# Last gate projection by 128-channel columns, between seven-product steps of the out-projection's left half

## The chip, the cores and the metric

One core of a Trainium2 chip runs the whole program. The metric is device time in microseconds (us). The kernel before took 2122.43 us, the median of three runs (2122.37 to 2122.54). A profile of one execution stands beside the times.

## What is computed

A decoder trunk of two layers on 256 tokens of width 2048, all in float32. The part that the change touches is, per layer:

```python
h = _rmsnorm(x, attn_norm_g[l])
proj = h @ w_in[l]
q, k, v, gate_b, gate_c, conv_in = jnp.split(proj, splits, axis=-1)   # each 1024 wide
...
attn = (_rmsnorm(attn, subln_g[l]) * (1.0 - lam_init)).reshape(B, S, ATTN_WIDTH)
conv = gate_b * _short_conv(gate_c * conv_in, conv_w[l])
x = x + jnp.concatenate([attn, conv.astype(attn.dtype)], axis=-1) @ w_out[l]
hm = _rmsnorm(x, mlp_norm_g[l]) @ w_up[l]
x = x + jnp.square(jax.nn.relu(hm)) @ w_down[l]
```

## The kernel before

**Numbers in two halves.** Every float32 operand of a matmul is split into a rounded high half and the rest: ScalarE (ACT) copies `hi`, VectorE (DVE) subtracts to get `lo`. A product is then three matmuls (`TERMS`: hi by hi, hi by lo, lo by hi). Weights come from HBM into `raw` buffers by DMAs that SyncE (SP) issues, and are split as they arrive (lines 322 and 323, `whi` and `wlo`). There are four `raw` buffers (`RAW`) and three of each of `whi` and `wlo` (`wpool`). `Weights.take` writes the next weight tiles into the program three jobs (`AHEAD`) before they are used.

**The order.** TensorE's order is the order in which the Python code issues matmuls. The other engines' orders come from a scheduler, and buffers of a pool are handed out in the order of the code. Each engine's queue is strictly in order: an instruction that waits holds up all behind it. `work` holds background pieces (attention, norms) that advance at each `tick` between matmuls.

**The mixer of a layer.** q, k and v are projected, then `gate_c` and `conv_in` in four groups of 256 channels each (`linear_t`, line 433), with the attention of the second half of the heads between them. Then comes `gate_b` (the last gate, tiles `gb`), also in four groups of 256 channels: for each, 32 matmuls over eight blocks of channels with 512 columns (high and low half of the activations at once) and 256 columns, twice. `joined` and `gate` add the two halves, multiply by the convolution and store both halves of the result in `cat[2]` and `cat[3]`. `cat[0]` and `cat[1]` hold the attention.

**The out-projection.** `BySeven.project` runs once for the left 1024 output columns (`g` = 0) and once for the right. The contraction of 2048 rows goes in eight pairs of 128-row blocks (pairs 0 to 3 are attention, 4 to 7 the gated convolution). An ordinary pair is two chunks of 12 matmuls with 512 columns. For the pairs in `GATED` (4 and 5) the 2x2 blocks are multiplied with seven products instead of eight: 21 matmuls instead of 24. Such a step needs sums of the activations (`sums_of`, tiles `sv`, `sf`) and sums of the weights (`jobs`: tile `w7t` for the sums, `w7b`, `w7x`, `w7y` for the split halves), and four additional accumulators, which are added into `x` at the end. The MLP's first loop (line 1172, `upc`, and line 1215, `pr`) has long had columns of 128 channels and seven-product steps in turn.

**PSUM.** Eight banks: `mm2` is two tiles of two banks, `bank` is three tiles of one bank, `av` is one bank.

Of the kernel before, what the change touches and what calls it, by code (L numbers as in the profile page):

```python
# [38 lines left out]
GATED = (0, 1)  # L39
# [83 lines left out]
def trunk(ctx: ExitStack, tc: tile.TileContext, x, w_in, w_out, conv_w, q_norm_g, k_norm_g,  # L123
# [142 lines left out]
    def load_bias(l, bpool, bias, setup):  # L266

        if l == 0:
            yield from small_setup(*setup)
        revs = []  # L270
        for j in range(2):
            rev = bpool.tile([P, NH, S], F32, tag="b", name=f"rev{l}{j}")
            src = by_dist_d[j * NH:(j + 1) * NH, 0:S]
            nc.gpsimd.dma_start(
                rev, bass.AP(src.tensor, src.offset, [[1, P], [REL, NH], [1, S]]))
            revs.append(rev)
        yield 4 if l else 12
        for h in range(0, NH, 2):
            for j in range(2):
                late(nc.scalar.activation(bias[:, j * NH + h:j * NH + h + 2],  # L280
                                          revs[j][:, h:h + 2, ::-1], AF.Copy))
            yield 2
# [24 lines left out]
    class Weights:  # L307
# [80 lines left out]

        def turned(self, w, col):
            for i in range(D // P // 4):  # L390
                self.plain(w, 4 * P * i, col, 4)

# [217 lines left out]
    def attention(l, qT, kT, kL, v, h0, dst, bias, tmp, pace):  # L610
# [9 lines left out]
        def unit(i):  # L620
# [19 lines left out]
            for t in range(NT):  # L640
                W = (t + 1) * P
                for m in range(2):
                    nc.vector.tensor_tensor_reduce(
                        out=s[:, m, OFF[t]:OFF[t] + W], in0=sc[t][:, m],
                        in1=bias[:, 2 * h + m, S - W:], op0=ALU.add, op1=ALU.max, scale=1.0,
# [60 lines left out]
            yield 12 * pace  # L706
            for t in range(NT):
# [4 lines left out]
                tp3 = tp.rearrange("p (h c) -> p h c", c=P)  # L712
                hi = parts[:, 0, :, t * P:(t + 1) * P]
                nc.scalar.activation(hi, tp3, AF.Copy, scale=s_gain[:, l:l + 1])
                nc.vector.scalar_tensor_tensor(
                    parts[:, 1, :, t * P:(t + 1) * P], tp3, s_gain[:, l:l + 1], hi.bitcast(F32),
                    op0=ALU.mult, op1=ALU.subtract)
# [17 lines left out]
    def in_parts(dst, j, value):  # L735

        hi, lo = (dst.open()[:, i, 2 * j:2 * j + 2] for i in range(2))
        nc.scalar.activation(hi, value, AF.Copy)
        nc.vector.tensor_sub(lo, value, hi.bitcast(F32))
        dst.ready = j == 1  # L740

    def gate(q, acc, cv, dst, y):
        g = joined(acc, f"gb{q}")
        nc.vector.tensor_mul(y, g, cv[:, q * 2:q * 2 + 2])
        in_parts(dst, q % 2, y)
# [5 lines left out]
    class BySeven:  # L751
# [3 lines left out]
        def __init__(self, l, bpool, weights):  # L755
            self.l, self.pool, self.weights = l, bpool, weights
            n = D // (4 * P)
            seven = [n + q for q in GATED]
            plain = [i for i in range(2 * n) if i not in seven]


            self.orders = []
            for g in range(2):
                chunks = (2 * g, 2 * g + 1)
                order = [(n, i) for n in chunks for i in plain[:2]]
                for i, j in zip(plain[2:], seven):
                    order += [("seven", j), ("pair", i)][::-1 if g else 1]
                order += [("pair", i) for i in plain[2 + len(seven):-2]]
                order += [(n, i) for n in chunks for i in plain[-2:]]
                self.orders.append(order)  # L770
            self.sums = []

        def sums_of(self, q, y):

            if len(self.sums) % 2 == 0:
                room = self.pool.tile([P, 2, 2, 4, P], F32R, tag="b", name="sf")
                self.sums += [room[:, 0], room[:, 1]]
            a11, a21, a12, a22 = (y[:, k, t * P:(t + 1) * P] for k in range(2) for t in range(NT))
            v = wide(f"sv{q}").rearrange("p (s c) -> p s c", c=P)
# [4 lines left out]
            hi, lo = (self.sums[GATED.index(q)][:, part] for part in range(2))  # L784
# [3 lines left out]
        def jobs(self, w, i, col):  # L788
# [8 lines left out]
            def two(pool, tag, name, src):  # L797

                room = pool.tile([P, 2, 2, CH], F32R, tag=tag, name=name)
# [3 lines left out]
            def plain():  # L803
# [9 lines left out]
                b11, b21 = two(self.pool, "b", "w7b", raws[0])  # L813
# [4 lines left out]
            def sums():  # L818
                left, right = mine["raw"]
                t = mine["t"] = self.pool.tile([P, 4, CH], F32, tag="b", name="w7t")  # L820
# [3 lines left out]
                made = two(apool, "a", "w7x", t[:, 0:2])  # L824
# [5 lines left out]
            def more():  # L830
                return two(apool, "a", "w7y", mine["t"][:, 2:4])
# [3 lines left out]
        def project(self, g, cat, norm, kpool, tmp):  # L835
            weights, order = self.weights, self.orders[g]
            both = [mm.tile([P, NT, CH], F32, tag="mm2", name=f"o{self.l}{2 * g + n}")
                    for n in range(2)]
            accs = [[acc[:, t] for t in range(NT)] for acc in both]
            prods = {2: accs[0][0], 4: accs[0][1], 3: accs[1][0]}  # L840

            def plain(i, n):
                hi, lo = weights.take()
                for j in range(2):
                    k = 2 * i + j
                    a = cat[k // KG]
                    while not a.ready:
                        work.tick()
                    for t in range(NT):
                        for m, (pa, pw) in enumerate(TERMS):  # L850
                            nc.tensor.matmul(  # L851
                                accs[n][t], a.ap[:, pa, k % KG, t * P:(t + 1) * P],
                                (hi, lo)[pw][:, j], start=(k == 0 and m == 0),
                                stop=(i == last and j == 1 and m == 2))
                    work.tick()

            def form(i, pa, a):
                q = i - D // (4 * P)
                if a >= S1:
                    return self.sums[GATED.index(q)][:, pa, a - S1]  # L860
                k, t = 2 * i + a // 2, a % 2
                return cat[k // KG].ap[:, pa, k % KG, t * P:(t + 1) * P]

            def seven(i, start, end):
                if start:
                    for n in (1, 5, 6):
                        prods[n] = bank(f"po{self.l}{g}{n}")
                    prods[7] = ps.tile([P, CH], F32, tag="av", name=f"po{self.l}{g}7", bufs=1)
# [3 lines left out]
                for n, a, b in ((1, A11, b11), (2, A12, b21), (3, S4, b22), (5, S1, t1),  # L872
                                (7, S3, t3), (6, S2, t2), (4, A22, t4)):
                    own = n in (1, 5, 6, 7)
                    for m, (pa, pw) in enumerate(TERMS):
                        nc.tensor.matmul(prods[n], form(i, pa, a), b[pw],
                                         start=(start and own and m == 0),
                                         stop=(end and own and m == 2))
# [4 lines left out]
            def onto(n):  # L883
                for t in range(NT):
                    nc.vector.tensor_add(xs[2 * g + n][:, t], accs[n][t], xs[2 * g + n][:, t])

            last = order[-1][1]
            steps = [i for what, i in order if what == "seven"]
            done = [j for j, (what, i) in enumerate(order) if what == 2 * g][-1]
            for j, (what, i) in enumerate(order):  # L890
                if what == "pair":
                    plain(i, 0)
                    plain(i, 1)
                elif what == "seven":
                    seven(i, i == steps[0], i == steps[-1])
                    if i == steps[-1]:

                        x11, x21, x12, x22 = (xs[2 * g + n][:, t]
                                              for n in range(2) for t in range(NT))


                        room = tmp.tile([P, 2, CH], F32, tag="ao", name="es", bufs=1)
                        e1, e2, e3 = room[:, 0], wide("e2"), room[:, 1]
                        e4 = kpool.tile([P, CH], F32, tag="kL", name="es4")
                        nc.scalar.activation(e1, prods[1], AF.Copy)
                        nc.vector.tensor_add(e2, prods[6], e1)
                        nc.vector.tensor_add(e4, prods[5], e2)
                        nc.vector.tensor_add(x22, prods[5], x22)
                        nc.vector.tensor_add(e3, prods[7], e2)
                else:  # L910
                    plain(i, what - 2 * g)
                    if j == done:
                        onto(0)
                        for x_, e in ((x11, e1), (x21, e3), (x12, e4), (x22, e3)):
                            nc.vector.tensor_add(x_, x_, e)
                        if g:
                            work.start(norm.chunk(2 * g, 2), 2)
            onto(1)
            if g:
                work.start(norm.chunk(2 * g + 1, 2))  # L920
                return
            for n in range(2):
                work.start(norm.chunk(n, 2), 4 * n + 2)


    def mixer(l, norm, loads):

        with ExitStack() as scope:
            biasp = scope.enter_context(tc.tile_pool(name="biasp", bufs=1))
# [14 lines left out]
            for q in range(AW // WC):  # L944
                weights.turned(w_in[l], 3 * AW + q * WC)
            by_seven = BySeven(l, bpool, weights)
            for g, order in enumerate(by_seven.orders):
                for what, i in order:
                    if what == "seven":
# [535 lines left out]
```

## Time and profile before

| | |
|---|---|
| median of 3 runs | 2122.43 us |
| the profiled execution's own time | 2122.24 us |
| its span, first to last instruction | 2120.4 us |
| around the span | 1.8 us |
| TensorE busy | 2115.1 us |
| VectorE busy | 1748.2 us |
| ScalarE busy | 1382.2 us |
| granted TensorE clock | 1.0 |

In the profiled execution `gate_b` of layer 0 starts at 253.2 us and ends at 297.6; the out-projection follows until 383.9. In layer 1 the same starts at 1307.7. The views give busy times per engine and stretch, groups of equal instructions with their mean duration, instructions in order of time, and each DMA's time from issue to landing. A matmul's recorded duration is longer than the distance to the next one, since matmuls overlap; distances between starts are what counts.

### The profile page before, as it was taken

To read this page: it belongs to the slowest core of one execution; us is meant where nothing else is said; L and a number is where in the kernel's file an instruction comes from. 1 tells how busy PE (TensorE), PEld (TensorE's weight loads), DVE (VectorE), ACT (ScalarE), POOL (GpSimd) and SP (SyncE) were. 2 spreads that over 40 slices of the span, in tenths; PEclk is the share of its full clock that TensorE was granted. 3 is DMA by queue.
4 is the path that set the end of the run, shared out by engine and by line. 5 is a ranking of instruction groups with operands and counts; after the bars stand their busy time and mean duration, and the time that the engine had idled before them with its cause. 6 is when DMAs were issued, how large, how long until landed. Compare 5 with 4: busy or idle time off the path is not lost.

```text
span 2120.4 us, 29268 instructions
## 1 busy us (share of the span) xinstructions
PE 2115.1 (100%) x10845; PEld 1807.6 (85%) x10845; DVE 1748.2 (82%) x2428; ACT 1382.2 (65%) x1838; POOL 159.2 (8%) x226
## 2 busy tenths in 40 slices
PE   9999999999999999999999999999999999999999
PEld 7888888888888888888888888888888888888887
DVE  6777678898888888799766776788988888888997
ACT  6776555676776776666566765557777677675664
POOL 3010100000000000011101101000000000000110
PEclk9999999999999999999999999999999999999999
DMA  8546666787777777788655565658877777777993
GB/s 279 175 154 205 193 194 191 251 257 226 230 233 233 230 236 230 248 299 293 213 169 182 162 212 179 199 169 267 258 229 235 231 232 233 231 229 261 319 309 104
DMA packets 297744, 476.02 MB, mean 224 GB/s; under 512 B 12707, under 2 KB 193781, under 8 KB 297600
## 3 DMA queue, kind: packets, MB, share of 16 engines
q1 hardware_dynamic: 269120, 406.76, 60.1%
q0 software_dynamic: 28288, 67.24, 9.9%
q8 instruction: 85, 1.39, 0.3%
q14 instruction: 59, 0.48, 0.1%
q10 hardware_dynamic: 192, 0.15, 0.0%
HBM read 440.52 MB, written 33.58 MB: 224 GB/s over the span
## 4 chain that ended last, share of the span: by engine, by line
PE 99%; ACT 1%; issue 0%; DVE 0%; DVEq 0%
PE upc L1172 31%; PE pr L1215 14%; PE dn L1296 8%; PE o L851 6%; PE ci L433 4%; PE gc L433 4%; PE gb L433 4%; PE k L408 4%; PE q L408 4%; PE v L408 4%; PE dn L1378 2%; PE dn L1215 2%; PE pr1r L1215 2%; PE pr0r L1215 1%; PE up L1172 1%; PE upw L1172 1%
## 5 line engine op out<-in xcount | busy, mean ns | idle before, releaser
L1172 PE MATMUL upc<-nT,uhi 128*128 128x512 f32 x1920 | 454.7, 389 | 0.0
L323 DVE TENSOR_TENSOR wlo<-raw,whi 128x1024 fp32r<-128x1024 f32 x258 | 311.8, 1222 | 156.9 <-ACT whi L322 85.6
L1172 PEld LDWEIGHTS upc<-nT,uhi 128*128 128x128 f32 x1920 | 360.3, 188 | 74.7
L322 ACT ACTIVATE whi<-raw 128x1024 fp32r<-128x1024 f32 x258 | 272.8, 1059 | 230.1 <-PE gb L433 28.0
L1036 DVE TENSOR_TENSOR ulo<-uraw,uhi 128x1024 fp32r<-128x1024 f32 x256 | 311.7, 1221 | 110.7 <-ACT f L1204 91.5
L1035 ACT ACTIVATE uhi<-uraw 128x1024 fp32r<-128x1024 f32 x256 | 270.6, 1057 | 157.8 <-PE upc L1172 137.5
L1172 PEld LDWEIGHTS upc<-nT,ulo 128*128 128x128 f32 x1920 | 246.2, 191 | 9.3
L1172 PE MATMUL upc<-nT,ulo 128*128 128x256 f32 x1920 | 249.1, 283 | 0.0
L1296 PE MATMUL dn<-whi,fb 128*128 128x512 f32 x496 | 156.5, 389 | 0.0
L851 PE MATMUL o<-whi,cat 128*128 128x512 f32 x384 | 122.0, 391 | 0.0
L1061 ACT ACTIVATE b2h<-draw 128x1024 fp32r<-128x1024 f32 x83 | 88.2, 1063 | 48.5 <-PE pr L1215 41.3
L322 ACT ACTIVATE whi<-uraw 128x1024 fp32r<-128x1024 f32 x62 | 65.9, 1062 | 81.8 <-PE dn L1296 66.0
L1296 PEld LDWEIGHTS dn<-whi,fb 128*128 128x128 f32 x496 | 93.1, 188 | 19.2
L1182 ACT ACTIVATE ev<-upc 128x512 f32<-128x512 f32 x120 | 72.0, 600 | 54.5 <-PE upc L1172 54.5
L1061 ACT ACTIVATE t24h<-t 128x1024 fp32r<-128x1024 f32 x83 | 88.3, 1063 | 22.8 <-PE pr L1215 15.9
L1062 DVE TENSOR_TENSOR t24l<-t,t24h 128x1024 fp32r<-128x1024 f32 x83 | 101.1, 1218 | 1.7
L1062 DVE TENSOR_TENSOR b2l<-draw,b2h 128x1024 fp32r<-128x1024 f32 x83 | 100.9, 1215 | 1.1 <-ACT b2h L1061 1.1
L1062 DVE TENSOR_TENSOR t13l<-t,t13h 128x1024 fp32r<-128x1024 f32 x83 | 101.0, 1217 | 0.7
L1075 DVE TENSOR_TENSOR t<-draw 128x1024 f32<-128x1024 f32 x83 | 101.1, 1218 | 0.3
L1061 ACT ACTIVATE t13h<-t 128x1024 fp32r<-128x1024 f32 x83 | 88.4, 1065 | 13.3 <-DVE t L1075 2.9
L1296 PE MATMUL dn<-wlo,fb 128*128 128x512 f32 x248 | 96.5, 389 | 0.0
L1215 PE MATMUL pr<-t13h,f 128*128 128x512 f32 x240 | 93.8, 391 | 0.0
(447 smaller groups left out, 4296.3 us busy)
## 6 DMA issues: line engine op xcount, KB each, us to landing
uraw<-in_w_up_dram SPq DMA_DIRECT2D x128, 1024.0 KB, 6.3
raw<-in_w_in_dram SPq DMA_DIRECT2D x191, 512.0 KB, 4.3
draw<-in_w_down_dram SPq DMA_DIRECT2D x174, 512.0 KB, 5.2
raw<-in_w_out_dram SPq DMA_DIRECT2D x64, 512.0 KB, 4.2
uraw<-in_w_down_dram SPq DMA_DIRECT2D x62, 512.0 KB, 5.7
raw<-in_w_down_dram SPq DMA_DIRECT2D x10, 1024.0 KB, 5.4
hid0p<-f POOLq DMA_DIRECT2D x19, 512.0 KB, 3.6
fb<-hid0p POOLq DMA_DIRECT2D x19, 512.0 KB, 7.5
```

The source lines that it names most:

```text
L322: pair = (nc.scalar.activation(hi, raw, AF.Copy), nc.vector.tensor_sub(lo, raw, hi.bitcast(F32)))
L323: nc.vector.tensor_sub(lo, raw, hi.bitcast(F32)))
L408: nc.tensor.matmul(acc[:, t], a.ap[:, pa, k % KG, t * P:(t + 1) * P], (hi, lo)[pw][:, j], start=(k == 0 and (pa, pw) == (0, 0)), stop=(k = ...
L433: nc.tensor.matmul(acc[:, f, 0] if part else acc[:, f], wt[:, k % 4, fs], a.ap[:, 0, k % KG] if part else a.ap[:, :, k % KG], start=(part ...
L851: nc.tensor.matmul(accs[n][t], a.ap[:, pa, k % KG, t * P:(t + 1) * P], (hi, lo)[pw][:, j], start=(k == 0 and m == 0), stop=(i == last and ...
L1035: pair = (nc.scalar.activation(hi, src, AF.Copy), nc.vector.tensor_sub(lo, src, hi.bitcast(F32)))
L1036: nc.vector.tensor_sub(lo, src, hi.bitcast(F32)))
L1061: keep(nc.scalar.activation(hi, src, AF.Copy))
L1062: keep(nc.vector.tensor_sub(lo, src, hi.bitcast(F32)))
L1172: nc.tensor.matmul(acc[:, 0] if part else acc, wt[part][:, k], a.ap[:, 0, k % KG] if part else a.ap[:, :, k % KG], start=(part == 0 and kh ...
L1215: nc.tensor.matmul(prods[n], f[:, pa, a], b[pw], start=(start and m == 0), stop=(stop and m == 2))
L1296: nc.tensor.matmul(prods[p], f[:, pa, 2 * k + t], b[pw][:, n], start=(p in starts and k == 0 and m == 0), stop=(stop and k == 1 and m == 2))
```

## The change

`gate_b` goes by columns of 128 channels (`c` 0 to 7): 16 matmuls with 512 columns and 16 with 256 for each, with two weight loads each of 1024 rows by 128 channels. Each column accumulates in one bank (`bank` for the first, `av` for all others). Between the columns stand the halves of seven-product steps of the out-projection's left half. Five pairs (0 to 4) of the left half now go by seven; the fifth (pair 4) follows the ordinary pair 5. Half `a` of a step has 12 matmuls, half `b` has 9. The order is the tuple `LEFT`. The right half keeps two such steps, of pairs 2 and 3 instead of 4 and 5. The sums of activations of pairs 0 to 3 are made at the end of each attention half, where the output now first goes through a copy (`ay`) in SBUF. The bias tile is cut in two, and its two buffers are used afterwards for `w7x` and `w7y`; `w7t` of the left half takes the buffer of `kL`, and the sums of pair 4 take two buffers of `tmp`.

```diff
-GATED = (0, 1)
+LEFT = (("c", 0), ("c", 1), ("a", 0), ("c", 2), ("b", 0), ("c", 3), ("a", 1), ("c", 4), ("b", 1),
+        ("c", 5), ("a", 2), ("c", 6), ("b", 2), ("c", 7), ("a", 3), ("b", 3), (0, 5), (1, 5),
+        ("a", 4), ("b", 4), (0, 6), (1, 6), (0, 7), (1, 7))
+SEVEN_LEFT = tuple(i for what, i in LEFT if what == "a")
+SEVEN_RIGHT = (2, 3)
...
+        def column(self, w, col):
+            def half(kh):
+                def make():
+                    raw = self.pool.tile([P, 8, P], F32, tag="raw", name="raw", bufs=RAW)
+                    nc.sync.dma_start(
+                        raw, w[kh * 8 * P:(kh + 1) * 8 * P, col:col + P].rearrange(
+                            "(k p) c -> p k c", p=P))
+                    return self.halves(raw)
+                return make
+            return [half(kh) for kh in range(2)]
...
+    def column_part(acc, acts, weights):
+        tiles = [weights.take() for _ in range(2)]
+        for part in range(2):
+            for kh, wt in enumerate(tiles):
+                for k in range(8):
+                    a = acts[kh * 2 + k // KG]
+                    nc.tensor.matmul(
+                        acc[:, 0] if part else acc, wt[part][:, k],
+                        a.ap[:, 0, k % KG] if part else a.ap[:, :, k % KG],
...
-                hi = parts[:, 0, :, t * P:(t + 1) * P]
-                nc.scalar.activation(hi, tp3, AF.Copy, scale=s_gain[:, l:l + 1])
+                y = wide(f"ay{h0}_{t}")
+                nc.scalar.activation(y, tp, AF.Copy, scale=s_gain[:, l:l + 1])
+                ys.append(y.rearrange("p (h c) -> p h c", c=P))
+                hi = parts[:, 0, :, t * P:(t + 1) * P]
+                nc.scalar.activation(hi, ys[t], AF.Copy)
+                nc.vector.tensor_sub(parts[:, 1, :, t * P:(t + 1) * P], ys[t], hi.bitcast(F32))
                 yield 2
+            for j in range(2):
+                sums_of(h0 // 2 + j, *(ys[t][:, 2 * j + k] for k in range(2) for t in range(NT)))
+                yield 2
...
+    def gate(c, acc, cv, dst, y):
+        ev = nat.tile([P, 2, S], F32, tag="wide", name=f"gb{c}")
+        nc.scalar.activation(ev, acc, AF.Copy)
+        nc.vector.tensor_add(y, ev[:, 0], ev[:, 1])
+        nc.vector.tensor_mul(y, y, cv[:, c])
+        hi, lo = (dst.open()[:, i, c % KG] for i in range(2))
+        nc.scalar.activation(hi, y, AF.Copy)
+        nc.vector.tensor_sub(lo, y, hi.bitcast(F32))
+        dst.ready = c % KG == KG - 1
...
+        def left(self, acts, cv):
+            weights, l = self.weights, self.l
+            while not self.cat[1].ready:
+                work.tick()
+            self.prods = prods = {}
+            def column(c):
+                acc = (ps.tile([P, CH], F32, tag="av", name=f"gb{l}{c}", bufs=1) if c else
+                       bank(f"gb{l}{c}"))
+                acc = acc.rearrange("p (h s) -> p h s", h=2)
+                column_part(acc, acts, weights)
...
+                gate(c, acc, cv, self.cat[2 + c // KG], y[:, c % 2])
+                if c % 2 and i in SEVEN_LEFT + SEVEN_RIGHT:
+                    self.sums_of(i, ...)
+            for j, (what, i) in enumerate(LEFT):
+                if what == "c":
+                    column(i)
+                elif what == "a":
+                    if start:
+                        banks()
+                    b11, b21, b22 = weights.take()
+                    self.t1, self.t3 = weights.take()
+                    self.product(1, i, A11, b11, start, end)
+                    self.product(2, i, A12, b21, start, not {"a", 0} & rest)
+                    self.product(3, i, S4, b22, start, not {"a", 1} & rest)
+                    self.product(5, i, S1, self.t1, start, end)
+                elif what == "b":
+                    t2, t4 = weights.take()
+                    self.product(7, i, S3, self.t3, start, end)
+                    self.product(6, i, S2, t2, start, end)
+                    self.product(4, i, A22, t4, start, not {"b", 0} & rest)
+                    if end:
+                        add = self.results(0)
+                else:
+                    opening = what == 1 and 8 not in prods
+                    if opening:
+                        prods[8] = ps.tile([P, CH], F32, tag="av", name=f"po{l}8", bufs=1)
+...
+                    self.pair(i, [(what, accs[what])], [(1, 1)] if opening else (),
+                              not {what, "b"} & rest)
+                    if j == len(LEFT) - 1:
+                        add()
+                        for n in range(2):
+                            for t in range(NT):
+                                nc.vector.tensor_add(xs[n][:, t], accs[n][t], xs[n][:, t])
...
-            biasp = scope.enter_context(tc.tile_pool(name="biasp", bufs=1))
+            biasp = scope.enter_context(tc.tile_pool(name="biasp", bufs=2))
...
-            for q in range(AW // WC):
-                acc = linear_t(f"gb{l}{q}", hT, weights)
-                gate(q, acc, cv, cat[2 + q // 2], ys[:, q])
-                if q in GATED:
-                    by_seven.sums_of(q, ys[:, q])
-
+            by_seven.left(hT, cv)
             mnorm = Norm(1, l)
-            for g in range(2):
-                by_seven.project(g, cat, mnorm, kpool, tmp)
+            for n in range(2):
+                work.start(mnorm.chunk(n, 2), 4 * n + 2)
+            by_seven.right(mnorm)
```

More of the change, by code (lines that the diff above doesn't have):

```diff
@@ L773, in sums_of @@
[L773 to L779, printed above, removed]
+            self.biasp, self.tmp = biasp, tmp
+            self.pairs = range(D // (2 * P))
+            plain = [i for i in self.pairs if i not in SEVEN_RIGHT]
@@ L795, in split, with two @@
                 return hi, lo
[L797 to L799 removed]
+            def two(room, src):
                 hi, lo = split(room[:, 0], room[:, 1], src)
@@ L874, in seven @@
                     own = n in (1, 5, 6, 7)
[L875 to L878, printed above, removed]
+                    self.product(n, i, a, b, start and own, end and own)
                     if n == 5:
@@ L881, in seven @@
                 work.tick()
[L883 to L889, printed above, removed]
-            for j, (what, i) in enumerate(order):
[L891 to L917, printed above, removed]
@@ L918, in project @@
-            onto(1)
[L919 to L923, printed above, removed]
+            for j, (what, i) in enumerate(order):
+                if what == "seven":
+                    seven(i, i == SEVEN_RIGHT[0], i == SEVEN_RIGHT[-1])
+                    if i == SEVEN_RIGHT[-1]:
+                        add = self.results(2)
+                    continue
+                chunks = range(2) if what == "pair" else (what - 2,)
+                self.pair(i, [(n, accs[n]) for n in chunks],
+                          starts if i == opening else (), i == last)
+                if j == done:
+                    onto(0)
+                    add()
+                    work.start(norm.chunk(2, 2), 2)
```

196 lines of the change are left out of this document (126 added, 70 removed).

## The prediction

> **What bounds the kernel now.** I read the page first: busy time and the chain that ended last.
>
> ```profile
> span 2120.4 us, 29268 instructions
> PE 2115.1 (100%) x10845; PEld 1807.6 (85%) x10845; DVE 1748.2 (82%) x2428; ACT 1382.2 (65%) x1838; POOL 159.2 (8%) x226
> ...
> PE 99%; ACT 1%; issue 0%; DVE 0%; DVEq 0%
> ```
>
> TensorE (PE) is the chain. It is idle for 5.3 us of the span, so there is little to win but its own work: the time follows the number of matmuls, until something makes PE wait. The second view, busy time by stretch, shows how near that is: gate_b of layer 0, the left half of its out-projection, and a piece of the MLP's first loop.
>
> ```profile
> core 0: us, PE busy (x) PEld busy (x) DVE busy (x) ACT busy (x) POOL busy (x), PEclk, DMA share, GB/s
> 253.00:297.00 44.00, 44.00 (x254) 38.84 (x254) 30.12 (x41) 22.74 (x27) 2.15 (x1) 1.00 0.59 189
> 297.00:340.00 43.00, 43.00 (x195) 35.74 (x194) 36.56 (x42) 22.02 (x27) 0.00 (x0) 1.00 0.61 195
> 450.00:550.00 100.00, 100.00 (x540) 86.85 (x539) 88.28 (x122) 70.99 (x82) 3.65 (x6) 1.00 0.77 236
> ```
>
> VectorE (DVE) has a third of its time free beside the gate and 15% beside the out-projection; a seven-product step costs DVE more than an ordinary pair, so the change spreads that load. In the MLP DVE is busy for 88% and PE still never stands: columns and seven-product steps in turn can run at PE's pace.
>
> **What goes.** PE's pace is the distance between starts, here of the gate (timeline) and of three ordinary matmuls:
>
> ```profile
> 253.18 3.82 PE L433 MATMUL gb<-nT,whi 128*128 128x512 f32 x16
> 256.83 2.08 PE L433 MATMUL gb<-nT,wlo 128*128 128x256 f32 x16
> 258.74 3.82 PE L433 MATMUL gb<-nT,whi 128*128 128x512 f32 x16
> ...
> 330.15 0.61 PE L851 MATMUL o<-whi,cat 128*128 128x512 f32 x2
> 330.60 0.39 PE L851 MATMUL o<-wlo,cat 128*128 128x512 f32 x1
> 330.83 0.61 PE L851 MATMUL o<-whi,cat 128*128 128x512 f32 x2
> ```
>
> 330.15 to 330.83 is 0.68 for three matmuls of 512 columns, 0.227 each. The left half goes from two seven-product steps to five, each with 21 matmuls instead of 24: 9 fewer per layer, 18 in all, 18 x 0.227 = **4.1 us saved**. The gate's matmuls stay the same in number and shape: 32 in 5.56 us (253.18 to 258.74), which is one column now. The right half keeps two steps.
>
> **What DVE must do.** Mean durations of one instruction (groups, shapes apart):
>
> ```profile
> L323 DVE TENSOR_TENSOR wlo<-raw,whi 128x1024 fp32r<-128x1024 f32 x258 | 311.8, 1222 | 156.9 <-ACT whi L322 85.6 <-issue 52.5 <-PE ci L433 6.5
> ...
> L322 ACT ACTIVATE whi<-raw 128x1024 fp32r<-128x1024 f32 x258 | 272.8, 1059 | 230.1 <-PE gb L433 28.0 <-issue 27.8 <-PE o L851 23.4
> ...
> L1182 ACT ACTIVATE ev<-upc 128x512 f32<-128x512 f32 x120 | 72.0, 600 | 54.5 <-PE upc L1172 54.5
> ...
> L1078 DVE TENSOR_TENSOR t<-t,draw 128x512 f32<-128x512 f32 x83 | 56.7, 684 | 0.0
> ...
> L1183 DVE TENSOR_TENSOR h<-ev 128x256 f32<-128x256 f32 x128 | 53.1, 417 | 0.0
> ...
> L1199 DVE TENSOR_TENSOR h<-h 128x128 f32<-128x128 f32 x60 | 17.0, 283 | 0.0
> ...
> 252.47 2.36 DVE L323 TENSOR_TENSOR wlo<-raw,whi 128x1024 fp32r<-128x1024 f32 x2 [3.21 <-issue]
> 254.75 0.68 DVE L447 TENSOR_TENSOR ci03w<-ci,ci03l 128x512 f32<-128x512 f32 x1
> ...
> 256.81 1.28 DVE L729 SCALAR_TENSOR_TENSOR cv<-gc03w,gains,cv 128x255 f32<-128x255 f32 x3 [0.58 <-ACT cv L727]
> ```
>
> Two splits take 2.28 from start to start, so instructions in a row overlap by 0.08 and cost 1.14, 0.60 (512), 0.34 (256), 0.20 (128). A column has two splits and three operations of 256 (add, gate, low half): 3.3. A step has three splits and five operations of 512: 6.4. Two columns and a step are 13.0 of DVE beside 2 x 5.56 + 21 x 0.227 = 15.9 of PE, 82%, under the 88% of the MLP loop. On ScalarE (ACT) they are 10 of 15.9. So no engine becomes the bound on average. In the attention stretch 8 sums of 128, 2 splits of 512 and 2 copies join per half, some 3 us of DVE, before a wait for `cat[1]` that had long been met: PE's order up to the gate is unchanged in the built program. The eight DVE additions into `x` at the left half's end (8 x 0.60) have 24 matmuls of the right half (5.4) before the first transpose reads them. I cost both at nothing; without that cover it would be 1 to 2 us each.
>
> **Where the new order makes PE wait.** In the built program I followed each buffer's previous user, from the first column's start t = 0. Steps a and b take 12 and 9 matmuls (2.7 and 2.0): c2 starts at 13.9, c4 at 29.8, a2 follows c5.
>
> First, a2. DVE's queue has, in both layers:
>
> ```
> cat <- y        low half of column 4, the first into cat[3]
> wlo <- raw      first half of column 6
> w7b <- raw      blocks of step 2
> ```
>
> The `w7b` of step 2 comes so late since its pool gives buffers out in the code's order, and `cat[3]`, opened after c4, is ahead of it. The `wlo` before it needs the buffer from which c5's low pass reads: free 8 matmuls of 256 columns before c5 ends, which is 8 x 1.91 / 16 = 0.96 (256.83 to 258.74 is 1.91 for 16). So `w7b` is done 1.22 + 1.14 - 0.96 = 1.4 after c5's end, plus some 0.1 for two handovers, and the step's second matmul, due at 0.23, is its first reader: **1.3 us of PE per layer**. It could be 0 if `w7b` were earlier, but in-order queues exclude that; 1.5 if handovers are slower.
>
> Second, c4. All columns but the first share the bank `av`, so c4 waits for the eviction of c3, and that stands in ACT's queue behind the split of c4's second half, which waits for a load. DVE's queue from the end of conv_in (t about 2.7, after a late `w7b`) to c2's second split has 4 splits, 7 of 512, 4 of the convolution (0.40 each, three in 1.28 above, overlapped alike) and 2 of 256: 11.1, so 13.8. That frees the raw buffer for step 1's second load; landed after 4.7, at 18.5. Then two sums, a `w7b`, a small sum and c3's second split: 3.7, so 22.2. Only now c4's second load may start, since there are four raw buffers. With its landing time L the rest is ACT's: split 1.06, `w7y` 1.06, 0.4, 0.6, eviction 0.60, in all 3.7: `av` is free at 25.9 + L, and c4 is due at 29.8. **The wait is L - 3.9.** The like chain ahead of c2 is shorter (c1's second split ends at 6.3; then L, a split, a `w7y`, the eviction: 2.7), so c2 waits L - 4.9.
>
> What is L? A column's load has 512 KB in 1024 rows of 512 bytes. No load of the trace has such rows in number. The nearest:
>
> ```profile
> DMA to landing us min/median/max: 3.4/4.2/4.9
> ...
> uraw<-in_w_up_dram SPq DMA_DIRECT2D x128, 1024.0 KB, 6.3
> raw<-in_w_in_dram SPq DMA_DIRECT2D x191, 512.0 KB, 4.3
> ```
>
> The first line is for `raw` in 253 to 300: a lone load of 512 KB in 512 rows lands after 3.4, one behind another after 4.9. `uraw` has as many rows as a column's load, and twice the bytes: 6.3. So L is between 3.4 (bytes count) and 6.3 (rows count); I take the middle, 4.8, since neither row is nearer. Below 3.4 there is no reason. c4 then waits 0.9, c2 0.
>
> The Trainium skill ("DMA: Bandwidth & Descriptors", Specifications) gives 512 bytes as the smallest transfer at line rate. By it L would be 4.2, c4 would wait 0.3, and the sum below would be 1.2 less. No row here shows it for 512 bytes; the two stretches above agree for 1 and 2 KB (0.59 at 189 GB/s, 0.61 at 195).
>
> **Sum.** Per layer 1.3 + 0.9 = 2.2, plus 0.1 per layer for switching between columns and steps: 4.6 lost, 4.1 saved, +0.5 on the profiled execution's 2122.24. That execution is 0.2 under the median of the runs, 2122.43, so the forecast is 2122.24 + 0.5 + 0.2 = **2122.9 us**.
>
> **Rivals.** (A) *No wait survives*: the MLP pattern holds here too.
>
> ```profile
> L1172 PE MATMUL upc<-nT,uhi 128*128 128x512 f32 x1920 | 454.7, 389 | 0.0
> ...
> ACT ev L1182 <- PE upc L1172: 54.5, 114, 0.9
> ```
>
> There the same single bank is evicted at once (ACT stands waiting for PE, 0.9 at most) and PE idles 0.0. Against it: there each group of blocks has buffers of its own, here `w7b` queues behind `cat[3]`. It gives 2122.4 - 4.1 = 2118.3; a little under 2118.2 only if columns run a trifle closer than 5.56.
>
> (B) *The column loads are slow* (the other side: slower). Every row of 512 bytes costs nearly what one of 1024 does. At L = 6.3 c4 waits 2.4, c2 1.4, and step 2's own late split about 1 more beside its 1.3: 6.1 per layer, 12.2 - 4.1 = +8.1, 2130.6. It passes 0.2% (4.2 us, about what a measurement of this kernel can tell from no change) when the two layers lose 8.3, so from 2 x (L - 3.9) + 2 x (L - 4.9) + 2.8 = 8.3 on, L = 5.8. For it: the MLP's 6.3, and 16384 such rows in a stretch. Against it: the DMA share is 0.6, far from full.
>
> The Trainium skill ("Perfetto Trace Analysis", Identifying Performance Opportunities) says that a gap that repeats on the engine that should be full can mean too few buffers for the next tile. By that rule every one of six columns in `av` would wait; here the MLP's 0.0 with the same bank disagrees, so it speaks for waits only where a load stands in between, as at c4 and c2.
>
> (C) *DVE falls behind* in the first 45 us, because it starts late after the sums of attention. Each us it is late moves c4 by one: 2 us in both layers make 4 more, 2127. This ends on the same side as (B).
>
> **Chances.** Forecast (waits at a2 and c4, within 2119.5 to 2126.5) 0.55; (A) 0.17; (B) 0.20; (C) 0.08. Faster by over 0.2%: a third of (A), 0.06. Slower by over 0.2%: (B), most of (C) and a little of the forecast's upper end, 0.29. Within 0.2%: 0.65. The range leaves out most of (A) and the worst of (B): 2119.3 to 2131; the forecast's own is 2119.5 to 2126.5.
>
> **What would show it.** PE's timeline: 64 matmuls of columns c0 and c1 without a gap, a gap of about 0.9 before c4, of 1.3 after the first matmul of the third step, both in each layer, and PE busy down by about 4 to 9 us. Loads of 512-byte rows land after about 4.8. The forecast is wrong if PE is idle no more than before (A), if column loads land after 6 and several columns start late (B), or if PE waits for DVE's splits where the loads had landed (C).

## The result, and the profile after

The changed kernel takes 2129.44 us, the median of seven runs (2128.54 to 2130.57); the kernel before took 2122.43 (2122.28 to 2122.73) beside it. The ratio is 1.0033, with a 95% interval of 1.0021 to 1.0044: slower by 7.0 us. The forecast was 2122.9. The profiled execution takes 2129.56.

The page of the changed kernel: the span, the busy times, and the chain that ended last, by engine.

```profile
span 2127.8 us, 29379 instructions
PE 2114.4 (99%) x10827; PEld 1805.0 (85%) x10827; DVE 1783.4 (84%) x2518; ACT 1402.2 (66%) x1880; POOL 171.3 (8%) x226
...
PE 92%; DVE 3%; DMA 2%; ACT 1%; issue 1%; DVEq 0%; ACTq 0%; SPq 0%
```

TensorE (PE) has its 18 matmuls less, but the chain now runs over VectorE (DVE), DMA and ScalarE (ACT) for some 6%. PE's busy time went down only by 0.7, not by 4.1, mostly since a matmul ahead of a wait is recorded to its end and the one behind a wait takes longer (8 x 0.27 = 2.2 of the 3.4 between them, as worked out below). So the loss is read from PE's timeline, here all of its rows with an idle note in the two stretches (start, duration, engine, line, tiles, shapes, count, then idle time and what ended it).

```profile
269.07 3.92 PE L417 MATMUL gb<-nT,whi 128*128 128x512 f32 x16 [0.65 <-ACT gb L774]
286.24 3.94 PE L417 MATMUL gb<-nT,whi 128*128 128x512 f32 x16 [0.92 <-ACT gb L774]
301.19 1.43 PE L884 MATMUL po<-w7b,cat 128*128 128x512 f32 x5 [1.26 <-DVE w7b L830]
322.91 0.50 PE L898 MATMUL po<-wlo,cat 128*128 128x512 f32 x1 [0.77 <-DVE wlo L327]
...
1326.55 3.93 PE L417 MATMUL gb<-nT,whi 128*128 128x512 f32 x16 [0.80 <-ACT gb L774]
1343.59 3.93 PE L417 MATMUL gb<-nT,whi 128*128 128x512 f32 x16 [0.85 <-ACT gb L774]
1358.80 1.43 PE L884 MATMUL po<-w7b,cat 128*128 128x512 f32 x5 [1.34 <-DVE w7b L830]
1380.80 0.50 PE L898 MATMUL po<-wlo,cat 128*128 128x512 f32 x1 [1.05 <-DVE wlo L327]
```

The same four places in both layers: c2, c4, step 2 (a2), and the first low half of pair 5, just behind column 7 and step 3. What a wait costs is more than its idle time. Around the third row, and behind the fourth:

```profile
299.54 0.39 PE L884 MATMUL po<-w7b,cat 128*128 128x512 f32 x1
301.19 1.19 PE L884 MATMUL po<-w7b,cat 128*128 128x512 f32 x4 [1.26 <-DVE w7b L830]
...
323.25 0.63 PE L898 MATMUL po<-whi,cat 128*128 128x512 f32 x2
```

From start to start it is 301.19 - 299.54 = 1.65, which is 1.42 over the pace of 0.227: the idle time and the 0.16 by which a record of 0.39 is longer than the pace. Behind a wait the next start comes late as well: 322.91 to 323.25 is 0.34 instead of 0.227, another 0.11. So a wait costs its idle time and about 0.27, taken here for all eight. The eight rows add up to 7.64 idle, and 7.64 + 8 x 0.27 = 9.8 us lost. By the stages it is a little more: from the first `gb` to the first `up` of a layer it took 131.11 and 131.12 before (253.18 to 384.29, 1307.71 to 1438.83), and takes 133.91 and 134.47 now (254.38 to 388.29, 1311.71 to 1446.18). That is 2.80 + 3.35 = 6.15 longer although 4.1 was saved, so 10.2 lost, 0.4 of it in gaps too short for a note. The other 1.2 of the span's 7.4 lie at the program's start (`gb` of layer 0 begins at 254.38 instead of 253.18), and belong to this execution alone, as the run "again" shows.

Why do these four stand still? The second view is busy time by stretch, from the first column on, and DVE's own waits in that stretch (what it waited for: us in total, times, longest).

```profile
254.38:300.00 45.62, 43.98 (x237) 37.32 (x235) 40.72 (x62) 27.85 (x37) 7.09 (x1) 1.00 0.65 192
```

```profile
DVE w7t L859 <- DMA raw<-in_w_out_dram: 3.6, 3, 1.6
...
DVE w7b L830 <- ACT w7b L829: 1.3, 1, 1.3
```

DVE (third engine of the row) is busy for 40.72 of 45.62 and idle for 4.9. Those 4.9 are these two waits: three times it stood at `w7t`, the first sum of a step's weights, which reads the step's second block before that load has landed, and once at `w7b`, the split of step 0's first block, for ACT's copy of that block, which had itself stood for its load. DVE has no other free time here.

### The profile page after: what moved, and what is told of

Its sections match the earlier page's. It is cut to its first block, busy times and chain, and to the rows that moved or that the text cites. A ratio compares the mean times of both kernels' runs of the same rounds, so it can differ in the third digit from the quotient of the medians.

```text
span 2127.8 us, 29379 instructions
## 1 busy us (share of the span) xinstructions
PE 2114.4 (99%) x10827; PEld 1805.0 (85%) x10827; DVE 1783.4 (84%) x2518; ACT 1402.2 (66%) x1880; POOL 171.3 (8%) x226
## 4 chain that ended last, share of the span: by engine, by line
PE 92%; DVE 3%; DMA 2%; ACT 1%; issue 1%; DVEq 0%; ACTq 0%; SPq 0%
PE upc L1296 31%; PE pr L1339 14%; PE dn L1420 8%; PE gc L465 4%; PE k L440 4%; PE q L440 4%; PE ci L465 4%; PE v L440 4%; PE o L898 3%; PE dn L1502 2%; DMA raw<-in_w_out_dram 2%; PE dn L1339 2%; PE po L898 2%; PE pr1r L1339 2%; PE pr0r L1339 1%; DVE wlo L327 1%
## 5 line engine op out<-in xcount | busy, mean ns | idle before, releaser
L327 DVE TENSOR_TENSOR wlo<-raw,whi 128x1024 fp32r<-128x1024 f32 x246 | 298.3, 1222 | 121.0 <-ACT whi L326 85.9
L326 ACT ACTIVATE whi<-raw 128x1024 fp32r<-128x1024 f32 x246 | 260.0, 1059 | 206.9 <-PE v L440 22.1
L1185 ACT ACTIVATE t24h<-t 128x1024 fp32r<-128x1024 f32 x83 | 88.2, 1063 | 22.5 <-PE pr L1339 15.9
L327 DVE TENSOR_TENSOR wlo<-uraw,whi 128x1024 fp32r<-128x1024 f32 x62 | 75.8, 1223 | 17.8 <-ACT whi L326 17.4
```

The lines of the kernel that those rows point to most:

```text
L326: pair = (nc.scalar.activation(hi, raw, AF.Copy), nc.vector.tensor_sub(lo, raw, hi.bitcast(F32)))
L327: nc.vector.tensor_sub(lo, raw, hi.bitcast(F32)))
L1185: keep(nc.scalar.activation(hi, src, AF.Copy))
```

## The experiments

Theory 1 as I went in: the waits come from in-order queues behind loads that the ring of four `raw` buffers issues late, at step 2 from the order of its `w7b`. Theory 2: rows of 512 bytes land slowly. Theory 3: DVE has too much to do. Each kernel is the changed kernel with one edit.

**A fifth buffer (five_raw).**

```diff
+        def room(self, shape):
+            self.loads += 1
+            if self.loads % 5 == 3:
+                return self.spare.tile(shape, F32, tag="ao", name="rawc", bufs=1)
+            return self.pool.tile(shape, F32, tag="raw", name="raw", bufs=RAW)
...
-                    raw = self.pool.tile([P, 8, P], F32, tag="raw", name="raw", bufs=RAW)
+                    raw = self.room([P, 8, P])
```

The loads of the left half's step blocks go through `room` in the same way.

> The left half's weight loads get a fifth buffer: every fifth of them lands in the tile `ao`, which the attention no longer needs by then. In the built program the `w7b` of step 2 also comes to stand one split earlier, ahead of the first split of c6. Changed kernel: 2129.4, with TensorE late by 4.8 in layer 0 and 5.3 in layer 1, at four places each (c2, c4, step 2, pair 5). Theory 1 (ring of four buffers and in-order queues): the waits at c2, c4 and pair 5 go and that of step 2 goes with its order, so 10.1 less: 2119.3, between 2118.3 and 2121. Theory 2 (rows of 512 bytes land slowly): a fifth buffer starts a load earlier by about one split only, half of the waits stay: about 2124. Theory 3 (VectorE has too much to do): the waits come back elsewhere, above 2127.

Measured 2118.82 (2118.41 to 2120.38), ratio 0.9983 (0.9974 to 0.9992): faster than both kernels, and 10.6 under the changed one. The page, and the same stretch of PE work:

```profile
span 2116.6 us, 29381 instructions
PE 2111.1 (100%) x10827; PEld 1803.8 (85%) x10827; DVE 1784.6 (84%) x2518; ACT 1402.8 (66%) x1880; POOL 187.5 (9%) x226
```

```profile
253.31:298.87 45.56, 45.56 (x248) 39.47 (x246) 44.88 (x64) 30.31 (x41) 12.52 (x1) 1.00 0.67 200
```

PE does not stand once in either layer's stretch, and the span is 3.8 under that before: the 4.1 of the 18 matmuls, nearly whole. In this stretch DVE never waits at `w7t` and is busy for 44.88 of 45.56: it uses the time in which it had stood, and gets further ahead of PE with it. So the work fits; what did not fit was the 4.9 of standing still. The edit changed one thing more: step 2's `w7b` stands one split earlier in DVE's queue. The next run and the last one, five_early, tell the buffer and the order apart.

**Step 2's blocks one job earlier (early2).**

```diff
                 column_part(acc, acts, weights)
+                if c == 4:
+                    weights.made.append(weights.jobs[len(weights.made)]())
```

> The block splits of step 2 (`w7b`) are written into the program one job earlier, ahead of the opening of cat[3], and stand on VectorE's queue ahead of the second split of c4 instead of behind the first of c6. Theory 1: the wait inside step 2 goes (1.57 in layer 0, 1.75 in layer 1), the others stay as they are: 2129.4 - 3.3 = 2126.1. Theory 3 (VectorE has too much to do): earlier blocks make other splits late by as much, less than 1 us is won: above 2128.4. Theory 2 (slow rows) says nothing on step 2 and expects as theory 1 here.

Measured 2123.68 (2122.01 to 2124.52), ratio 1.0004 (0.9995 to 1.0013), 5.8 better than the changed kernel instead of 3.3. PE's rows with idle notes in layer 0:

```profile
268.60 3.92 PE L417 MATMUL gb<-nT,whi 128*128 128x512 f32 x16 [1.12 <-ACT gb L774]
285.71 3.92 PE L417 MATMUL gb<-nT,whi 128*128 128x512 f32 x16 [0.91 <-ACT gb L774]
```

The wait of step 2 is gone, and pair 5's with it, which I had taken for separate; in layer 1 too (c2, c3 and c4 wait there, 1.12, 0.49 and 0.97). The trace shows why pair 5 is on time. In the changed kernel its first split is one of the two in the second row here, behind a `w7t` of step 4 that waits for a load:

```profile
319.29 0.69 DVE L859 TENSOR_TENSOR w7t<-raw 128x512 f32<-128x512 f32 x1 [2.89 <-DMA raw<-in_w_out_dram]
...
321.64 2.35 DVE L327 TENSOR_TENSOR wlo<-raw,whi 128x1024 fp32r<-128x1024 f32 x2
```

In early2 DVE stands nearly as long for the loads of step 4, now at `w7b`, but pair 5's first split is ahead of that in the queue (first row):

```profile
314.41 1.22 DVE L327 TENSOR_TENSOR wlo<-raw,whi 128x1024 fp32r<-128x1024 f32 x1
317.81 1.22 DVE L830 TENSOR_TENSOR w7b<-raw,w7b 128x1024 fp32r<-128x1024 f32 x1 [2.19 <-ACT w7b L829]
```

So this edit moved two splits in DVE's queue, and both waits went with the order; the loads of step 4 still come late.

**Long rows (longrows).**

```diff
+                    row, col = 2 * P * (2 * (i % 4) + kh), base + i // 4 * CH
                     nc.sync.dma_start(
-                        raw, w[kh * 8 * P:(kh + 1) * 8 * P, col:col + P].rearrange(
-                            "(k p) c -> p k c", p=P))
+                        raw.rearrange("p (k m) c -> p k (m c)", k=2),
+                        w[row:row + 2 * P, col:col + CH].rearrange("(k p) c -> p k c", p=P))
```

> Each column load fetches as many bytes, but in 256 rows of 2 KB instead of 1024 rows of 512 bytes (other columns of w_in, so the gate has other numbers). Instructions and their order stay. Theory 1: the column loads already land after 3.7 to 3.9 alone and 4.7 to 5.1 in a queue, against 3.4 and 4.9 of 1-KB rows before, so c2, c4 and pair 5 get at most 0.3 each back per layer: 2127.6 to 2129.4, the four places stay. Theory 2 (slow rows): the waits of c2, c4 and pair 5 go, 6.8 in both layers: 2122.6.

Measured 2130.68 (2130.28 to 2133.18), ratio 1.0041 (1.0028 to 1.0053): no better, and 1.3 above theory 1's range. The same eight places wait; c2 of layer 1 waits longer, 2.38. The landing times of the column loads in 253 to 300, of the changed kernel and then of this one:

```profile
DMA to landing us min/median/max: 3.7/4.5/5.1
```

```profile
DMA to landing us min/median/max: 3.7/4.2/4.9
```

A load of 512 KB lands alike in 1024 rows of 512 bytes and in 256 rows of 2 KB. Theory 2 is out. The page "DMA: Bandwidth & Descriptors" (Specifications) of the Trainium skill gives 512 bytes as the smallest transfer at line rate. The two rows agree in so far as 512 bytes are no slower than 2 KB; no run here has shorter rows.

**Less for DVE (light_dve).**

```diff
-                nc.vector.tensor_add(t[:, 2], t[:, 1], left[:, 0])
-                nc.vector.tensor_sub(t[:, 3], left[:, 1], t[:, 2])
...
-                return two(room, mine["t"][:, 2:4])
+                return two(room, mine["t"][:, 0:2])
```

> The second pair of weight sums of each step is left out (two VectorE instructions of 512, about 1.2 us per step, five steps on the left and two on the right per layer); the products that read them take the first pair, so the out-projection has other numbers. In the built program the `w7b` of step 2 then stands ahead of both splits of c6. Theory 1: the wait of step 2 goes with its order (3.3 in both layers), and the chains ahead of c2 and c4 get shorter by up to 1.2, which takes 0.6 to 1.1 from each; pair 5 keeps half of its wait: 2121.5 to 2124.5. Theory 3 (VectorE has too much to do): all waits go, 2119.3. Theory 2 (slow rows): only the wait of step 2 goes, 2126.

Measured 2119.83 (2118.66 to 2121.35), ratio 0.9986 (0.9978 to 0.9995). That is next to theory 3's number and below theory 1's range. The stretch, and what DVE waited for in it:

```profile
253.55:299.11 45.56, 45.56 (x248) 39.47 (x247) 40.35 (x58) 28.79 (x39) 4.83 (x1) 1.00 0.69 204
```

```profile
DVE w7t L859 <- DMA raw<-in_w_out_dram: 3.2, 2, 2.7
DVE w7b L830 <- ACT w7b L829: 2.0, 2, 1.4
```

DVE still stands for 5.2, but now it has the time, and PE does not wait in layer 0 (and once in layer 1, 1.07 at c3). Part of the gain is order, since step 2's `w7b` moved here too: early2 reached 2123.7 by order alone, and the 3.9 from there to 2119.8 came with the lighter load. So neither theory has it alone: late loads cost next to nothing where DVE has slack (here), and a DVE that is 98% full costs nothing where loads are on time (five_raw). Together they make PE wait.

**One buffer for one load: c4's second half (spare_one), and step 0's second block (spare_first).** The edit is that of five_raw with another condition, one of these for each kernel:

```diff
-            if self.loads % 5 == 3:
+            if self.loads in (14,):      # spare_one
+            if self.loads in (6,):       # spare_first
```

> Only one load per layer, the second half of column 4, gets a buffer of its own (the tile `ao`); all others keep the ring of four. In the built program the `w7b` of step 2 still stands behind the low half of column 4, but now ahead of both splits of c6 instead of behind the first. Theory 1 (each wait is one load that the ring issues late, with the eviction or the block split queued behind its split): c4's wait goes (1.22 and 1.15), step 2's goes with the order and pair 5's with it, as early2 showed (2.6 and 3.1); only c2's of about 1.0 per layer stays: 2118.8, the time of five_raw, and 2.1 more, 2120.9. Rival (the loads as a whole are too slow, so one buffer only moves the wait to the next column): c5 or c6 wait instead, above 2124.

> Again only one load per layer gets a buffer of its own (the tile `ao`), and the earliest possible one: the second block of the first seven-product step (step 0), for which VectorE stood still at `w7t` (0.47 in layer 0 of the changed kernel). All later loads keep the ring of four. Theory 1 in its first form (each of the four places has a late load of its own): only c2's wait goes, about 1.0 per layer, the other three stay: 2129.2 - 2.0 = 2127. Theory 1 in its new form (the first late load makes VectorE late, VectorE with some 90% of its time taken can't make it up, and so each later buffer comes free late and its load is issued late): without the first delay c4, step 2 and pair 5 lose most of their waits as well: 2119.5, between 2118.5 and 2121.

spare_one: 2122.38 (2121.07 to 2123.47), ratio 0.9999 (0.9990 to 1.0008), between theory 1's 2120.9 and the rival's 2124. Layer 0:

```profile
268.28 3.96 PE L426 MATMUL gb<-nT,whi 128*128 128x512 f32 x16 [1.01 <-ACT gb L783]
298.36 1.45 PE L894 MATMUL po<-w7b,cat 128*128 128x512 f32 x5 [0.48 <-DVE w7b L839]
```

c4's wait is gone in both layers, so it was that one load, with the eviction in the queue behind its split. No later column waits instead. In layer 1 only c2 waits, 1.23. But in layer 0 step 2 keeps a part of its wait, although its `w7b` here stands ahead of both splits of c6 and waits for neither: DVE had stood at the `w7t` of that step (its load was issued at 283.00 and landed after 5.7), and worked with hardly a pause from there to the `w7b` at 297.08:

```profile
288.76 0.69 DVE L869 TENSOR_TENSOR w7t<-raw 128x512 f32<-128x512 f32 x1 [1.11 <-issue]
...
297.08 1.22 DVE L839 TENSOR_TENSOR w7b<-raw,w7b 128x1024 fp32r<-128x1024 f32 x1
```

spare_first: 2123.24 (2121.97 to 2125.32), ratio 1.0002 (0.9993 to 1.0011), between both expectations (2127 and 2119.5). Layer 0, PE and then DVE at `w7t`:

```profile
275.79 3.92 PE L426 MATMUL gb<-nT,whi 128*128 128x512 f32 x16 [0.51 <-ACT gb L783]
284.67 3.93 PE L426 MATMUL gb<-nT,whi 128*128 128x512 f32 x16 [0.30 <-ACT gb L783]
299.36 1.43 PE L894 MATMUL po<-w7b,cat 128*128 128x512 f32 x5 [0.76 <-DVE w7b L839]
```

```profile
256.56 0.69 DVE L869 TENSOR_TENSOR w7t<-rawc,raw 128x512 f32<-128x512 f32 x1 [2.40 <-DMA raw<-in_w_out_dram]
290.27 0.69 DVE L869 TENSOR_TENSOR w7t<-raw 128x512 f32<-128x512 f32 x1 [2.19 <-DMA raw<-in_w_out_dram]
```

c2 and pair 5 start on time, c4 and step 2 wait less, and c3 waits instead (the first row). But the edit did not take the first lateness away: DVE stands 2.40 at step 0, now for the step's first block, which stayed in the ring (issued at 251.80, landed after 4.7). c2 is on time all the same, since with one load out of the ring its own second load is issued at 259.01, 5.4 after the first column's start, and no longer behind c1's second split, 8.3 after it. So c2's wait, like c4's, was one load issued late. Step 2's `w7b` and pair 5's split stand earlier here too, as in early2, and at step 2 the ring is late anew (2.19). How much of the other waits comes from a first delay that is handed on I can't say from this run.

**The eviction on DVE (dve_evict).**

```diff
-        ev = nat.tile([P, 2, S], F32, tag="wide", name=f"gb{c}")
-        nc.scalar.activation(ev, acc, AF.Copy)
-        nc.vector.tensor_add(y, ev[:, 0], ev[:, 1])
+        nc.vector.tensor_copy(y, acc[:, 0])
+        nc.vector.tensor_add(y, acc[:, 1], y)
```

> The eviction of a column's bank goes from ScalarE (one copy of 512) to VectorE (a copy of 256 and an addition of 256 that reads the other half); four buffers, as in the changed kernel. In the built program the next column's split stands on VectorE between the copy and the addition. Theory 1 (the bank comes free late because its eviction stands in an in-order queue behind a split that waits for its load): the queue is another one but the load is the same, and the addition comes a split (1.14) and itself (0.42) later: c2 and c4 wait some 1.2 longer each, about 2134. Rival (ScalarE itself is late, whatever it waits for): without the eviction on ScalarE c2 and c4 start on time, 2125.

Measured 2142.47 (2141.11 to 2144.71), ratio 1.0095 (1.0082 to 1.0109). The direction is theory 1's, and the rival's 2125 is out. The size and the places are not theory 1's: c2 waits 4.6, c3, c5 and c7 wait, c4 doesn't. So the run speaks against ACT as the late one, and confirms no more of theory 1. The bank's second reader now stands behind a split of column 3 whose load lands only at 267.2, and behind `w7y`.

**The changed kernel again (again).**

> The changed kernel as it is, once more. In its first profile the first `tpn` transposes started at 12.83 us, against 11.50 in the kernel before and 11.46 to 11.84 in the four kernels since, whose instructions up to the first attention half are the same. Theory: those 1.2 us at the start belonged to that one execution; here `tpn` starts between 11.4 and 11.9, the eight waits are as before (10.1 together) and the profiled execution takes about 2128.5. Rival (the program's start is slower): 12.8 again.

Measured 2128.98 (2127.96 to 2130.52), ratio 1.0032 (1.0020 to 1.0043). The first `tpn` starts at 11.48 and layer 0's `gb` at 253.47, so the 1.2 us at the start were that one execution's. Seven of the eight waits are there (c2 of layer 0 starts without an idle note, c2 of layer 1 waits 1.74 instead of 0.80): step 0's second block is issued 0.55 after the first column's start in both profiles of layer 0, but landed after 4.7 there and 3.6 here, so the wait at c2 depends in part on how long a load happens to take. Step 2 is steady: 1.33 and 1.33, after 1.26 and 1.34.

**Both remedies (five_early)**, the edits of five_raw and early2 together.

> The fifth buffer and the earlier blocks of step 2 together. Theory 1: five_raw left no wait of over 0.25 us in this stretch, so nothing more can be won: 2118.8, within 0.8. Theory 3 (VectorE has too much to do): a different order shows waits that five_raw hides by luck, 2120 to 2122.

Measured 2118.49 (2118.09 to 2119.31), ratio 0.9981 (0.9973 to 0.9990), with no wait in the stretch either. With the fifth buffer the earlier blocks add nothing that can be told from five_raw. Against early2 (2123.68), with the same earlier blocks, the buffer gives 5.2; so of the changed kernel's loss the earlier order alone gives back about half, and the buffer the rest.

## Why the prediction was off, by its steps

The range held the time; the forecast of +0.5 did not hold the +7.0, nor did the forecast's own bounds, 2119.5 to 2126.5. The range reached up to 2131 for rival (B), slow rows, which longrows rules out, so that it held the time is luck as far as the mechanism goes. By its steps:

- **18 matmuls, 4.1 saved: right.** With all waits gone (five_raw) the span is 3.8 shorter. From the first `gb` to the first `up` a layer then takes 129.16 and 129.15 (253.31 to 382.47, 1305.88 to 1435.03), 1.96 less than before: half of the 4.1, less the 0.1 set for switching. The sums of attention and the additions into `x`, costed at nothing, cost nothing that shows.
- **c2, predicted 0: wrong.** Idle 0.65 and 0.80 (with 0.27 each, 0.9 and 1.1 lost). L was 3.7, shorter than the 4.8 assumed, so by the formula there should have been even less. What failed is the other term, c1's second split ending 6.3 after the first column's start (the first row is ACT's):

```profile
256.27 1.06 ACT L829 ACTIVATE w7b<-raw 128x1024 fp32r<-128x1024 f32 x1 [2.49 <-DMA raw<-in_w_out_dram]
257.36 1.23 DVE L830 TENSOR_TENSOR w7b<-raw,w7b 128x1024 fp32r<-128x1024 f32 x1 [1.32 <-ACT w7b L829]
258.50 0.68 DVE L479 TENSOR_TENSOR ci03w<-ci,ci03l 128x512 f32<-128x512 f32 x1
259.66 0.69 DVE L859 TENSOR_TENSOR w7t<-raw 128x512 f32<-128x512 f32 x1 [0.47 <-DMA raw<-in_w_out_dram]
...
261.47 1.22 DVE L327 TENSOR_TENSOR wlo<-raw,whi 128x1024 fp32r<-128x1024 f32 x1
```

  It ended at 262.69, which is 8.3 after 254.38, 2.0 late. The chain begins with `ci03w`, at 4.1 instead of 2.7: step 0's `w7b` ahead of it waits for ACT's copy, and ACT for the load. That is 1.4 of the 2.0. Another 0.5 is the wait of the first sum for the next load; I had counted the sums as work alone.
- **c4, predicted 0.9: the number right (1.2 and 1.1), by errors that nearly cancel.** Its load was issued at 24.6 (278.98 - 254.38), not 22.2; but it landed after 3.8, not 4.8, and c4 itself was due 0.9 later, since c2 had waited. That the eviction waits behind the split of one load was right: spare_one.
- **Step 2, predicted 1.3: right in place, nearly in size (1.5 and 1.6), and for the most part in cause.** The blocks do stand too late in DVE's queue (early2). But DVE itself was late at the split ahead of them as well:

```profile
291.01 0.69 DVE L859 TENSOR_TENSOR w7t<-raw 128x512 f32<-128x512 f32 x1 [1.59 <-DMA raw<-in_w_out_dram]
...
298.78 1.22 DVE L327 TENSOR_TENSOR wlo<-raw,whi 128x1024 fp32r<-128x1024 f32 x1
299.92 1.22 DVE L830 TENSOR_TENSOR w7b<-raw,w7b 128x1024 fp32r<-128x1024 f32 x1
```

  From 291.01 to this `w7b` no row of DVE has an idle note: it works off what had piled up in the 1.59. The 1.59 was handed on from c4: that block's load was issued at 285.57, when c4's late second split had freed the buffer, and landed after 5.4. c5's low pass gives the buffer free at about 297.62 + 0.96 = 298.58, so without that backlog the split at 298.78 could have started at most 0.2 earlier, and the one in layer 1 at most 0.5 (1356.39 instead of 1354.96 + 0.96). The low pass, as predicted, accounts for the rest. The backlog shows by itself in spare_one, where it leaves 0.48.
- **Pair 5, predicted nothing: missed, 1.0 and 1.3.** Its split stands in DVE's queue behind a sum of step 4 that waits for a load (2.89); where it stands ahead, in early2, it is on time. The prediction follows no queue that far.
- **No engine becomes the bound on average: the term that was mis-sized.** I set 13.0 of DVE against 15.9 of PE, 82%, for two columns and a step. The first 45 us are no average: three steps must be prepared in the time of six columns and two steps, with the last convolution and the sums of pair 4 beside them. The trace has 40.72 of DVE there beside 45.62 - 2.6 = 43.0 of PE without its waits (2.6 is what those at c2, c4 and the first part of step 2's lost in it), 95%, and no room for another 4.9 of standing still. With a few us of free time the waits at `w7t` cost next to nothing, as in light_dve. Rival (C), DVE behind, was therefore a part of the cause, and had been given 0.08.
- **Rival (B), slow rows: ruled out** (longrows). **Rival (A), 2118.3: the time that the order gives once a fifth buffer feeds it.**
- **The sum:** predicted 4.6 lost, of which c4 and step 2 are 4.4. The trace has 9.8: 2.0 from c2, 2.3 from c4, 3.1 from step 2 and 2.4 from pair 5. PE's busy time, expected 4 to 9 lower, fell by 0.7 for the reason given with the page.

## What to carry to other kernels

Check an engine's load over the stretch where the change starts, with all that must be ready ahead of time in it, and not over the steady pattern; here VectorE, at 95%, had no room left for 4.9 of standing still. In an in-order queue an instruction that reads a load directly (here a sum of raw weights) is a wait and not only work: look up when its load can be issued, which the ring of buffers decides, and what stands behind it. One more buffer, here a tile that had fallen free, turned +7.0 into -3.8. An edit of one buffer or one instruction can also move others in the built queues, so compare their order before the gain is put down to the edit alone.

## What the runs showed of the hardware

The granted clock in dve_evict, by stretch (the last three numbers are PEclk, DMA share, GB/s), and PE's row at the wait:

```profile
267.00:271.70 4.70, 0.10 (x1) 0.01 (x1) 4.70 (x7) 2.06 (x3) 1.26 (x1) 0.93 0.74 211
271.70:278.00 6.30, 6.28 (x15) 5.00 (x16) 6.30 (x13) 1.94 (x3) 0.00 (x0) 0.51 0.47 148
278.00:284.00 6.00, 5.69 (x33) 4.70 (x32) 4.54 (x8) 3.28 (x4) 0.00 (x0) 1.00 0.61 177
...
1336.00:1340.00 4.00, 3.86 (x10) 3.11 (x11) 4.00 (x7) 1.57 (x3) 0.00 (x0) 0.57 0.70 228
```

```profile
271.73 6.76 PE L417 MATMUL gb<-nT,whi 128*128 128x512 f32 x16 [4.62 <-DVE y L774]
```

After 4.62 of idle time the 16 matmuls take 6.76 instead of some 3.9: the clock is at half for the next 6 us, some 3 us lost. In layer 1, after 4.64, they take 5.44: the clock is 0.57 over 4 us, some 1.7 lost. So a wait of that length costs about 2 to 3 us more than it lasts; the longest wait in these stretches of the other runs, 2.38 in longrows, left the clock at 1.00. The Trainium skill ("TensorE: Matmul & The Clock Gate", Part 1: The HAM clock gate) says that TensorE drops to half its clock after an idle window of about 3.4 us; these rows agree.
